# One decoder layer on one core: the first modulation columns, the emptying of banks and the FFN's modulation sums rearranged

## The chip, the core and the metric

The kernel runs on one core of a Trainium2 chip. The metric is the time of the core in microseconds of the device, as the median of several runs; lower is better. One execution is also profiled, and every row below is from that one.

## What is computed

One layer over 512 tokens of width 1024, in float32. A vector c gives six modulation vectors by one product with `w_mod` (1024 x 6144):

```python
mod = silu(c) @ w_mod + b_mod           # sh_m, sc_m, gt_m, sh_f, sc_f, gt_f
h = rms_norm(x, g_mix_norm) * (1 + sc_m) + sh_m
proj = h @ w_in                         # 12 slices: q, k, v of two mixers, an indexer, two gates
o_a = dsa_attention(...)                # each query keeps the 128 keys that the indexer scores highest
o_b = moba_attention(...)               # two blocks of 256 keys
merged = sigmoid(gate_a) * (o_a @ w_br_dsa) + sigmoid(gate_b) * (o_b @ w_br_moba)
x = x + gt_m * (merged @ w_out)
h = rms_norm(x, g_ffn_norm) * (1 + sc_f) + sh_f
x = x + gt_f * ((silu(g) * u) @ w_down) # g, u = halves of h @ w_gate_up; inner width 2816
```

## The kernel before

Every large product is made of three passes on TensorE in a rounded float32 format: high x high, high x low and low x high, where an operand's high part is its rounded copy (made by ScalarE) and its low part the difference (made by VectorE). Weights come from HBM into one of three `st` buffers, always through the queue of SyncE (SP), which takes its transfers in order and waits in order. A weight chunk is 256 rows by 512 columns (24 products of 512 columns, one unit of each half of the chunk); it is cast and split two chunks ahead of its use.

**The opening.** It is written out by hand, in one fixed order for each engine. x comes in four tiles of 128 tokens; each is squared and summed, scaled by its reciprocal root and turned by TensorE (`turn`), one 128-column slice into each of seven banks `xps`. The columns of `w_mod` for the first slice are summed over their 1024 rows: ScalarE takes the first two blocks (`first_products`), VectorE adds further ones (`add_up`), TensorE takes those that `direct` names and then the sum of VectorE (`sum_up`), all into two columns `pc` of one bank, column 1 the scale and column 0 the shift. VectorE makes `acol` (scale) and `mcol` (shift) of them, ScalarE makes the high part of the first slice (`high(0)`), and the products of the first slice begin (`first_group`). From slice 1 on a loop does the same once for each slice k, with the products of slice k-1 ahead of it. `unused_products(n)` issues n products of the identity with itself, of 384 columns, whose result nobody reads; they write columns 128 to 511 of the bank that holds `pc`. `keep` copies a turned slice out of its bank.

**The body.** After the opening a planner in Python (`Clocks`, `step`, `pump`) decides at build time in which order everything else is issued. The products of weight chunks follow a fixed list; each group of four chunks fills four banks, and `fin` (of `v_done`, `raw_done`, `gate_done` and others) empties a bank at the group's last chunk. Side work (rotary tables, indexer, top-k, attention heads, modulation) consists of generators in `tasks`; `step()` runs after every three products (`main3`) and issues each task's next piece if the planner's clocks say that its inputs are ready and that its engines are not more than `slack` ahead of TensorE. `arriving` is the planner's guess of when a transfer lands. `prep` casts and splits a weight chunk.

**The FFN's modulation.** `columns_task` makes four vectors of 512 modulation values as columns (128 partitions x 4 each), with `mod_columns`: `column_sums` accumulates on VectorE into one tile of 128 x 512, `halves` splits it, and TensorE sums over partitions with the tile's 128-column pieces as weights and two columns of ones as the moving operand: eight products of 2 columns. `norm_task` reads the columns first when it prepares the FFN's input.

`out_units` holds the second half of the product with `w_out`; after each tile's last product `residual` empties the bank on VectorE and `norm_task` is spawned.

Of the kernel before, what the change touches and what calls it, by code (L numbers as in the profile page):

```python
# [25 lines left out]
P = 128  # L26
# [87 lines left out]
def layer(ctx, tc, x, vecs, w_mod, w_in, gvecs, w_br_dsa, w_br_moba, w_out, w_gate_up, w_down, cosh, sinh, cosi, sini, out):  # L114
# [6 lines left out]
    wp = ctx.enter_context(tc.tile_pool(name="wp", bufs=3))  # L121
    sm = ctx.enter_context(tc.tile_pool(name="sm", bufs=2))
    pp = ctx.enter_context(tc.tile_pool(name="pp", bufs=1, space=PS))

    NB = {"H": 4, "O": 4, "K": 4, "V": 2, "g": 16, "gu": 2, "s": 3, "pT": 2, "cg": 2}
    uid = [0]
# [161 lines left out]
    with tc.manual_schedule(engines=engines):  # L288
# [13 lines left out]
        junk = t("V", [P, D])  # L302
        xnT = [t("O", [P, 4, S]) for _ in range(2)]
        sums = [None] * NK
        direct = {(0, 1): (6, 7), (0, 0): (4, 5, 6, 7), (1, 1): (6, 7), (1, 0): (6, 7)}

        def blocks(k, m):

# [16 lines left out]
                    ve.scalar_tensor_tensor(dst(j % 2), src(j), cs[:, j:j + 1], dst(j % 2), op0=ALU.mult, op1=ALU.add)  # L325
            ve.tensor_tensor(out=dst(0), in0=dst(0), in1=dst(1), op=ALU.add)

        def sum_up(k, pc, ms=(1, 0)):

            for m in ms:  # L330
                for n, j in enumerate(direct.get((k, m), ())):
                    te.matmul(pc[:, m:m + 1], strips[k][:, m, j, :], cs[:, j:j + 1], start=not n, stop=False)
                te.matmul(pc[:, m:m + 1], sums[k][:, 0, m, :], one, start=(k, m) not in direct, stop=True)

        def high(k, src):
# [40 lines left out]
        def rstd(i, more):  # L376
            ve.tensor_scalar(rs[i], ssx[:, i:i + 1], more, None, op0=ALU.add)
            ge.tensor_tensor(out=rs[i], in0=rs[i], in1=mhalf[:, 0:1], op=ALU.pow)

        for i in range(NT - 1):  # L380
            se.activation(junk, xs[i], AF.Square, scale=D ** -0.5, accum_out=ssx[:, i:i + 1])
            rstd(i, EPS)
            if i < NT - 2:
                scale(i)
                turn(i, range(NK - 1))
                unused_products(3)
        se.activation(junk[:, :512], xs[3][:, :512], AF.Square, scale=D ** -0.5, accum_out=ssx[:, 3:4])
        ve.tensor_tensor_reduce(out=junk[:, 512:], in0=xs[3][:, 512:], in1=xs[3][:, 512:], op0=ALU.mult, op1=ALU.add,
                                scale=1.0 / D, scalar=EPS, accum_out=ssx[:, 4:5])
        rstd(3, ssx[:, 4:5])  # L390
        scale(2)
        scale(3)
        turn(2, range(NK - 1))
        turn(3, (3, 4, 5, 6, 0, 1, 2))
        unused_products(2)
        first_products(0, 1)
        add_up(0, 1)
        sum_up(0, pc, (1,))
        first_products(0, 0)
        add_up(0, 0)  # L400
        sum_up(0, pc, (0,))
        unused_products(6)
        parts = weights_hi(0, (slice(0, 512), slice(512, 512 + N_Q)))
        next(parts)
        keep(3, se.copy)
# [2 lines left out]
        ve.scalar_tensor_tensor(acol[:, 0, 0:1], pc[:, 1:2], gmix[:, 0:1], bmg[:, 0:1], op0=ALU.mult, op1=ALU.add)  # L408
        keep(5, ve.tensor_copy)
        ve.tensor_scalar(mcol[:, 0:1], pc[:, 0:1], bm[:, 0:1], None, op0=ALU.add)  # L410
        high(0, xps[0])
        keep(6, ve.tensor_copy)
        weights_lo(0, slice(0, 512))
# [71 lines left out]
    def spawn(gen, slack=2.0, rank=2, on=busy):  # L485
        tasks.append([gen, (), slack, on, rank])
        tasks.sort(key=lambda task: task[4])

    def step():

        moved = False
        while True:
            hit = False
            for wait in (0.0, 0.15):
                for task in list(tasks):
                    fill = task[4] == 3
                    if wait and (hit or not fill):
                        continue
                    while task in tasks:
                        now = ck.at[PE]  # L500
                        if max(ck.at[e] for e in task[3]) > now + task[2]:
                            break
                        limit = max(now, ck.at[DVE] + 0.12 + wait) if fill else now
                        if not all(w is not None and w <= limit for w in map(when, task[1])):
                            break
                        hit = True
                        try:
                            task[1] = next(task[0]) or ()
                            if not isinstance(task[1], tuple):
                                task[1] = (task[1],)  # L510
                        except StopIteration:
                            tasks.remove(task)
                        if fill:
                            break
            if not hit:
                return moved
            moved = True
# [14 lines left out]
    def need_room(tag):  # L532
        pump(lambda: free[tag])

    def main3(*args):
        mm3(*args)
        step()

    def group(srcs, n, accs_of, mm, order, fin, need=(), change=None):

        accs = {}
        nk = 2 * len(srcs)
        chunks = []
        for c, src in enumerate(srcs):
            def unit(w, ks, js, last, c=c):
                if not accs:
                    accs.update(accs_of())
                for a, b in ([(k, j) for j in js for k in ks] if last else [(k, j) for k in ks for j in js]):
                    mm(accs[b], w[0][:, a], w[1][:, a], 2 * c + a, b, c == 0 and a == 0, 2 * c + a == nk - 1)
                    if last and a == ks[-1]:  # L550
                        fin(b, accs[b])
                        done(accs[b])

            last = c == len(srcs) - 1
            h = (len(order) + 1) // 2
            parts = [((0, 1), order[:h]), ((0, 1), order[h:])] if last else [((0,), order), ((1,), order)]
            units = [lambda w, p=p, unit=unit, last=last: unit(w, p[0], p[1], last) for p in parts]
            chunks.append((lambda src=src, n=n: wload(src, 2, n), units, need, change))
        return chunks

    def drive(chunks, ws, ahead=2):
        sts = {}

        def load(c):
            if c < len(chunks) and chunks[c][0]:
                need_room("st")
                sts[c] = chunks[c][0]()

        def prep(c):
            if c < len(chunks) and chunks[c][0]:  # L570
                st = sts.pop(c)
                if chunks[c][3]:
                    chunks[c][3](st)
                uid[0] += 1
                h, l = [wp.tile(list(st.shape), F32R, name=f"w{q}_{uid[0]}", tag="w" + q) for q in "hl"]
                se.copy(h, st)
                yield h
                ve.tensor_tensor(out=l, in0=st, in1=h.bitcast(F32), op=ALU.subtract)
                done(st)
                ws[c] = h, l  # L580
            load(c + 1)

        load(ahead)
        for c, (load_of, units, need, _) in enumerate(chunks):
            pump(lambda: all(f in ready for f in need) and (not load_of or c in ws))
            for u, unit in enumerate(units):
                unit(ws.get(c))
                if u == 0:
                    spawn(prep(c + ahead), slack=4.0, rank=-1, on=(DVE,))
                    step()  # L590
            ws.pop(c, None)
# [349 lines left out]
    def mod_columns(col0):  # L941

        tile, sums = yield from column_sums(col0, "K")
        parts = yield from halves(sums)
        done(tile)
        yield parts + (room("pstr"),)
        pc = ps("tr", (P, 4, 2))
        for j in range(4):
            for n, part in enumerate(parts):
                te.matmul(pc[:, j, :], part[:, j * P:(j + 1) * P], oner.to_broadcast([P, 2]), start=n == 0, stop=n == 1)  # L950
        j0 = col0 // P
        ve.tensor_tensor(out=mcol[:, j0:j0 + 4], in0=pc[:, :, 0], in1=bm[:, j0:j0 + 4], op=ALU.add)
        done(pc, *parts)

    def mod_rows(acc, col0, tag):

# [14 lines left out]
    def columns_task():  # L971
        yield "idx"
        for part in range(4):
            yield from mod_columns(3 * D + part * 512)
        ve.tensor_scalar(acol[:, 1, :], mcol[:, 32:40], 1.0, None, op0=ALU.add)
        ve.tensor_tensor(out=acol[:, 1, :], in0=acol[:, 1, :], in1=gffn, op=ALU.mult)

# [36 lines left out]
    def br_done(br, half):  # L1014
        def fin(f, acc):
            if not br and not half and not f:
                pump(lambda: len(free["K"]) == 4)
                merged.extend(t("K", [P, 4, S], F32R) for _ in range(4))
            j = 8 * br + 4 * half + f
            pump(lambda: f"gate{j}" in ready)  # L1020
            ve.tensor_tensor(out=gates[j], in0=acc, in1=gates[j], op=ALU.mult)
            if not br:
                spawn(merge(half, f), slack=0.5, rank=0)
            if half and f == 3:
                done(*outs[br])
        return fin
# [131 lines left out]
    def out_units():  # L1158
        units = []
        accs = {}  # L1160
        for i in range(NT):
            for k2 in range(NK // 2):
                def unit(_, i=i, k2=k2):
# [5 lines left out]
                    for k in (2 * k2, 2 * k2 + 1):  # L1169
                        mh, ml = mk(k, i)  # L1170
                        pump(lambda: len(wo) > k)
                        main3(accs[i], mh, ml, wo[k][0][:, 0], wo[k][1][:, 0], k == 0, k == NK - 1)
                    if k2 == NK // 2 - 1:
                        spawn(norm_task(i, residual(accs[i], gtm, i, 1)), slack=4.0, rank=-0.1 * i)
                        done(accs[i])
                        if i == NT - 1:
                            done(*gtm, *(q for hl in wo for q in hl), *merged)
                units.append(unit)
        return units

# [198 lines left out]
```

## Time and profile before

| | |
|---|---|
| median of 3 runs | 797.36 us (797.09 to 797.89) |
| the profiled execution | 797.7 us, of which 795.9 us lie between its first and last instruction |
| mean granted TensorE clock | 0.997 |
| busy share | TensorE 98%, VectorE 60%, ScalarE 46% |
| moved from and to HBM | 100.59 MB, mean 126 GB/s |

The span is what the rows below count in, from the first instruction on. A clock of 1.00 is 2.4 GHz, one of 0.50 is 1.2 GHz. Busy times of TensorE are no measure of its pace, since its products overlap: two products that start 0.23 us apart are each shown as 0.39 us long.

### The profile page before, as it was taken

The numbers are of one execution on the slowest core, as the hardware profiler recorded it, in microseconds if no ns is written. First come the engines' busy times: TensorE is split into PE (matmuls) and PEld (weight loads), VectorE is DVE, ScalarE is ACT, GpSimd is POOL, SyncE is SP. The second block draws the span as 40 slices with busy tenths as digits, with TensorE's granted clock in tenths as the row PEclk, the third lists the DMA queues.
The fourth block names the chain that finished last, engine by engine and source line by source line (L and its number), as shares of the span: only waits on it lengthen the run. The fifth ranks groups of instructions, "written<-read, shape, count | busy, mean of one in ns | idle before, by whom it ended". The sixth has DMA issues, their size and how long they took to land.

```text
span 795.9 us, 10081 instructions
## 1 busy us (share of the span) xinstructions
PE 781.0 (98%) x3743; PEld 648.2 (81%) x3743; DVE 477.4 (60%) x879; ACT 363.5 (46%) x763; POOL 29.1 (4%) x32
## 2 busy tenths in 40 slices
PE   5999999999999999999999999999999999999998
PEld 5887788787888788888888988888888888888886
DVE  4874979998799638638857365233333333644542
ACT  5763579898576777334434323223332322211210
POOL 2000012110020000000000000000000000000000
PEclk9999999999999999999999999999999999999999
DMA  9947343321144444634520176332332332433311
GB/s 323 342 140 225 127 156 83 130 76 58 54 132 142 149 140 158 206 106 141 164 93 20 34 215 207 106 106 90 96 106 86 99 88 71 133 107 109 129 54 53
DMA packets 78036, 100.59 MB, mean 126 GB/s; under 512 B 5980, under 2 KB 46244, under 8 KB 77988
## 3 DMA queue, kind: packets, MB, share of 16 engines
q1 hardware_dynamic: 77988, 99.96, 39.9%
q8 instruction: 29, 0.48, 0.2%
q14 instruction: 19, 0.16, 0.1%
HBM read 97.85 MB, written 2.10 MB: 126 GB/s over the span
## 4 chain that ended last, share of the span: by engine, by line
PE 96%; ACT 2%; DVE 1%; DMA 0%; issue 0%; POOL 0%; SPq 0%; DVEq 0%; ACTq 0%
PE psacc L107 62%; PE pstr L107 16%; PE pspv L107 9%; PE pss L107 9%; DMA O<-in_x_dram 0%; ACT sqj L107 0%; ACT V L107 0%; ACT g L107 0%; ACT H L107 0%; DVE pT L107 0%; DVE score L107 0%; DVE O L107 0%; DVE wl L107 0%; ACT s L107 0%; DVE s L107 0%
## 5 line engine op out<-in xcount | busy, mean ns | idle before, releaser
L107 DVE TENSOR_TENSOR wl<-st,wh 128x1024 fp32r<-128x1024 f32 (+1 forms) x120 | 145.0, 1208 | 123.5 <-ACT wh L107 122.5
L107 ACT CAST wh<-st 128x1024 fp32r<-128x1024 f32 (+1 forms) x120 | 124.4, 1038 | 178.9 <-PE psacc L107 66.7
L107 PE MATMUL psacc<-H,wh 128*128 128x512 f32 x576 | 181.8, 397 | 0.0
L107 PE MATMUL psacc<-wh,H 128*128 128x512 f32 x384 | 130.9, 408 | 3.0 <-ACT H L107 2.1
L107 PEld LDWEIGHTS psacc<-H,wh 128*128 128x128 f32 x576 | 106.8, 188 | 22.9 <-issue 1.4
L107 PE MATMUL psacc<-H,wl 128*128 128x512 f32 x288 | 112.3, 390 | 0.0
L107 PEld LDWEIGHTS psacc<-wh,H 128*128 128x128 f32 x384 | 72.2, 189 | 20.3 <-ACT H L107 2.7
L107 PE MATMUL psacc<-wl,H 128*128 128x512 f32 x192 | 71.9, 395 | 0.0
L107 PEld LDWEIGHTS psacc<-H,wl 128*128 128x128 f32 x288 | 54.1, 188 | 11.6
L107 PE MATMUL pstr<-H,wh 128*128 128x512 f32 (+1 forms) x176 | 54.3, 390 | 0.0
L107 PEld LDWEIGHTS psacc<-wl,H 128*128 128x128 f32 x192 | 36.8, 192 | 7.5 <-issue 1.0
L107 POOL TENSOR_TENSOR m<-m,mhalf 128x4 f32<-128x4 f32 (+1 forms) x24 | 27.3, 1136 | 403.4 <-DVE m L107 355.8
L107 PE MATMUL psacc<-wh,K 128*128 128x512 f32 x128 | 39.8, 389 | 0.0
L107 PE MATMUL psacc<-O,wh 128*128 128x512 f32 x128 | 39.4, 389 | 0.0
L107 PEld LDWEIGHTS pstr<-H,wh 128*128 128x128 f32 (+1 forms) x176 | 32.3, 183 | 7.6
L107 ACT ACTIVATE s<-s,att 128x128 f32<-128x128 f32 (+3 forms) x64 | 34.2, 561 | 2.0 <-DVE att L107 2.0
L107 PE MATMUL pstr<-H,wl 128*128 128x512 f32 (+1 forms) x88 | 34.3, 389 | 0.0
L107 DVE TENSOR_TENSOR s<-psacc,s 128x512 f32<-128x512 f32 x12 | 8.3, 692 | 40.9 <-PE psacc L107 38.7
L107 PEld LDWEIGHTS psacc<-wh,K 128*128 128x128 f32 x128 | 24.0, 188 | 5.1 <-DVE g L107 0.2
L107 PEld LDWEIGHTS psacc<-O,wh 128*128 128x128 f32 x128 | 24.0, 188 | 5.0
L107 DVE TENSOR_TENSOR st<-st,cg 128x1024 f32<-128x1024 f32 x22 | 26.8, 1218 | 0.0
L107 PEld LDWEIGHTS pspv<-pT,V 128*128 128x128 f32 x160 | 21.9, 190 | 6.0 <-DVE O L107 2.5
(236 smaller groups left out, 1342.4 us busy)
## 6 DMA issues: line engine op xcount, KB each, us to landing
st<-in_w_gate_up_dram SPq DMA_DIRECT2D x88, 256.0 KB, 3.2
st<-in_w_in_dram SPq DMA_DIRECT2D x36, 512.0 KB, 3.6
K<-in_w_mod_dram SPq DMA_DIRECT2D x12, 1024.0 KB, 6.5
st<-in_w_down_dram SPq DMA_DIRECT2D x22, 512.0 KB, 3.6
K<-in_w_mod_dram SPq DMA_DIRECT2D x16, 512.0 KB, 6.2
st<-in_w_in_dram SPq DMA_DIRECT2D x16, 256.0 KB, 4.1
st<-in_w_mod_dram SPq DMA_DIRECT2D x8, 512.0 KB, 3.7
O<-in_x_dram SPq DMA_DIRECT2D x4, 512.0 KB, 4.8
```

Source lines behind the costliest of these rows:

```text
L107: inst = f(*args, **kw)
```

## The change

In the opening: fourteen unused products go ahead of x, two instead of three follow each of the first two tiles, the two after the last tile and the six after the sums go, and four stand behind the first shift (`mcol`), ahead of `high(0)`. One more block of the first scale column is summed by TensorE (`direct`), and the direct products of that column are issued ahead of the turning of tiles 2 and 3.

In the body: at a group's last chunk side tasks may run 1 us less far ahead (`held_back`); after a bank's last product `step()` comes behind the bank's emptying, in `group` and in `out_units`; `prep` waits, in the plan, for its weights' landing; `merge` gets a slack of 1.5 in place of 0.5.

In `mod_columns`: the ones are the weights (two columns) and the two halves the moving operand, so two products of 512 columns give the sum as a row; ScalarE copies the row out, one transfer writes it to HBM and another reads it back into the four columns of `mcol`. The bias is added once, after the fourth part, by one instruction that the plan puts at least 8 us behind the landing that it guesses.

```diff
-        direct = {(0, 1): (6, 7), (0, 0): (4, 5, 6, 7), (1, 1): (6, 7), (1, 0): (6, 7)}
+        direct = {(0, 1): (5, 6, 7), (0, 0): (4, 5, 6, 7), (1, 1): (6, 7), (1, 0): (6, 7)}
...
-        def sum_up(k, pc, ms=(1, 0)):
+        def sum_direct(k, pc, m):
+            for n, j in enumerate(direct.get((k, m), ())):
+                te.matmul(pc[:, m:m + 1], strips[k][:, m, j, :], cs[:, j:j + 1], start=not n, stop=False)
+
+        def sum_up(k, pc, ms=(1, 0), begun=False):
...
+        unused_products(14)
         for i in range(NT - 1):
...
-                unused_products(3)
+                unused_products(2)
...
         scale(3)
+        sum_direct(0, pc, 1)
         turn(2, range(NK - 1))
         turn(3, (3, 4, 5, 6, 0, 1, 2))
-        unused_products(2)
         first_products(0, 1)
         add_up(0, 1)
-        sum_up(0, pc, (1,))
+        sum_up(0, pc, (1,), begun=True)
         first_products(0, 0)
         add_up(0, 0)
         sum_up(0, pc, (0,))
-        unused_products(6)
...
         ve.tensor_scalar(mcol[:, 0:1], pc[:, 0:1], bm[:, 0:1], None, op0=ALU.add)
+        unused_products(4)
         high(0, xps[0])
...
+    held_back = [0.0]
...
-                        if max(ck.at[e] for e in task[3]) > now + task[2]:
+                        if max(ck.at[e] for e in task[3]) > now + task[2] - held_back[0]:
...
     def main3(*args):
         mm3(*args)
-        step()
+        if not emptied_next[0]:
+            step()
...
+                held_back[0] = 1.0 if last else 0.0
                 for a, b in ([(k, j) for j in js for k in ks] if last else [(k, j) for k in ks for j in js]):
+                    emptied_next[0] = last and a == ks[-1]
                     mm(accs[b], w[0][:, a], w[1][:, a], 2 * c + a, b, c == 0 and a == 0, 2 * c + a == nk - 1)
-                    if last and a == ks[-1]:
+                    if emptied_next[0]:
+                        emptied_next[0] = False
                         fin(b, accs[b])
                         done(accs[b])
+                        step()
...
+                yield st
                 uid[0] += 1
...
-        parts = yield from halves(sums)
+        hi, lo = yield from halves(sums)
+        yield hi, lo, room("pstr")
+        pc = ps("tr", (2, 512))
+        te.matmul(pc, oner.to_broadcast([P, 2]), hi, start=True, stop=False)
+        te.matmul(pc, oner.to_broadcast([P, 2]), lo, start=False, stop=True)
+        done(hi, lo)
+        yield pc
+        row = sums[0:1, :]
+        se.copy(row, pc[0:1, :])
+        done(pc)
+        yield sums
+        j0 = col0 // P
+        turned = dp.tile([1, 512], F32, name=f"turned{j0}")
+        nc.sync.dma_start(turned, row)
+        nc.sync.dma_start(mcol[:, j0:j0 + 4], turned.rearrange("o (a p) -> p (o a)", p=P), allow_slow_non_contiguous=True)
+        arriving(mcol, 512)
         done(tile)
-        yield parts + (room("pstr"),)
-        pc = ps("tr", (P, 4, 2))
-        for j in range(4):
-            for n, part in enumerate(parts):
-                te.matmul(pc[:, j, :], part[:, j * P:(j + 1) * P], oner.to_broadcast([P, 2]), start=n == 0, stop=n == 1)
-        j0 = col0 // P
-        ve.tensor_tensor(out=mcol[:, j0:j0 + 4], in0=pc[:, :, 0], in1=bm[:, j0:j0 + 4], op=ALU.add)
-        done(pc, *parts)
...
+        landed = ck.ready[mcol.tensor.name][0] + 8.0
+        yield lambda: landed
+        ve.tensor_tensor(out=mcol[:, 24:40], in0=mcol[:, 24:40], in1=bm[:, 24:40], op=ALU.add)
...
-                spawn(merge(half, f), slack=0.5, rank=0)
+                spawn(merge(half, f), slack=1.5, rank=0)
...
-                        main3(accs[i], mh, ml, wo[k][0][:, 0], wo[k][1][:, 0], k == 0, k == NK - 1)
+                        (mm3 if k == NK - 1 else main3)(accs[i], mh, ml, wo[k][0][:, 0], wo[k][1][:, 0], k == 0, k == NK - 1)
...
                             done(*gtm, *(q for hl in wo for q in hl), *merged)
+                        step()
```

## Rows read from the trace of the kernel before

**Rows 1.** The page: busy time by engine, and the chain that ended last.

```profile
PE 781.0 (98%) x3743; PEld 648.2 (81%) x3743; DVE 477.4 (60%) x879; ACT 363.5 (46%) x763; POOL 29.1 (4%) x32
...
PE 96%; ACT 2%; DVE 1%; DMA 0%; issue 0%; POOL 0%; SPq 0%; DVEq 0%; ACTq 0%
```

**Rows 2.** Busy time by stretch: engines in order, then clock, DMA share, GB/s.

```profile
19.40:22.80 3.40, 3.36 (x8) 2.61 (x9) 3.37 (x7) 3.40 (x7) 0.00 (x0) 0.54 1.11 369
...
100.00:200.00 100.00, 99.24 (x515) 81.83 (x514) 89.58 (x233) 84.93 (x254) 15.49 (x11) 1.00 0.31 98
```

**Rows 3.** Waits of TensorE over the span: total us, times, longest.

```profile
PE pstr L107 <- DVE m L107: 4.5, 1, 4.5
...
PE psacc L107 <- ACT H L107: 2.1, 2, 1.9
PE psacc L107 <- DVE s L107: 1.0, 1, 1.0
PE psacc L107 <- ACT g L107: 0.8, 1, 0.8
```

**Rows 4.** Timeline of TensorE in the opening: start, us, what, idle before.

```profile
10.60 1.06 PE L107 MATMUL psacc<-identr,O 128*128 128x128 f32 x4
...
12.97 1.04 PE L107 MATMUL psacc<-identr,O 128*128 128x128 f32 x8
...
16.00 0.36 PE L107 MATMUL pstr<-one,gu 128*128 128x1 f32 x2
16.23 1.31 PE L107 MATMUL pstr<-identr 128*128 128x384 f32 x6
...
19.44 1.87 PE L107 MATMUL psacc<-wh,H 128*128 128x512 f32 x4 [1.91 <-ACT H L107]
...
23.66 1.08 PE L107 MATMUL psacc<-wh,H 128*128 128x512 f32 x4
24.58 0.40 PE L107 MATMUL pspv<-wl,H 128*128 128x512 f32 x1
...
28.11 1.19 PE L107 MATMUL psacc<-wh,H 128*128 128x512 f32 x4 [0.19 <-ACT H L107]
```

**Rows 5.** Timeline of VectorE in the opening, and one row of ScalarE.

```profile
11.47 1.14 DVE L107 SCALAR_TENSOR_TENSOR gu<-K,cs,gu 128x128 f32<-128x128 f32 x4
...
13.49 0.29 DVE L107 TENSOR_TENSOR gu<-gu 128x128 f32<-128x128 f32 x1
17.58 0.22 DVE L107 SCALAR_TENSOR_TENSOR acol<-pstr,cols,bmg 128x1 f32<-128x1 f32 x1 [3.79 <-PE pstr L107]
...
18.31 0.21 DVE L107 TENSOR_SCALAR mcol<-pstr,cols 128x1 f32<-128x1 f32 x1
...
23.38 0.43 DVE L107 TENSOR_TENSOR gu<-gu 128x256 f32<-128x256 f32 x1
...
18.61 0.78 ACT L107 ACTIVATE H<-pstr,mcol,acol 128x512 fp32r<-128x512 f32 x1 [3.31 <-DVE mcol L107]
```

**Rows 6.** Timeline of TensorE where one part's columns are summed.

```profile
158.92 1.03 PE L107 MATMUL pstr<-oner,gu 128*128 128x2 f32 x8
159.81 0.48 PE L107 MATMUL psacc<-wh,H 128*128 128x512 f32 x1
```

**Rows 7.** Timelines of ScalarE and VectorE around two waits of TensorE.

```profile
151.72 1.30 ACT L107 ACTIVATE g<-g,m 128x128 f32<-128x128 f32 x4
...
153.42 1.09 ACT L107 COPY g<-psacc 128x512 f32<-128x512 f32 x2
...
428.83 1.37 DVE L107 TENSOR_SCALAR pT<-pstr,acol,mcol 128x128 f32<-128x128 f32 x4 [1.35 <-PE pstr L107]
430.12 0.68 DVE L107 TENSOR_TENSOR s<-psacc,cg 128x512 f32<-128x512 f32 x1
```

**Rows 8.** Transfers by tile: count, KB each, median us from issue to landing.

```profile
K<-in_w_mod_dram SPq DMA_DIRECT2D x16, 512.0 KB, 6.2
...
out_dram<-V SPq DMA_DIRECT2D x7, 256.0 KB, 2.0
```

More of the change, by code (lines that the diff above doesn't have):

```diff
@@ L123, in layer @@
     pp = ctx.enter_context(tc.tile_pool(name="pp", bufs=1, space=PS))
+    dp = ctx.enter_context(tc.tile_pool(name="dp", bufs=1, space=bass.MemoryType.DRAM))
     NB = {"H": 4, "O": 4, "K": 4, "V": 2, "g": 16, "gu": 2, "s": 3, "pT": 2, "cg": 2}
@@ L326, in add_up @@
             ve.tensor_tensor(out=dst(0), in0=dst(0), in1=dst(1), op=ALU.add)
-        def sum_up(k, pc, ms=(1, 0)):
+        def sum_direct(k, pc, m):
+            for n, j in enumerate(direct.get((k, m), ())):
+                te.matmul(pc[:, m:m + 1], strips[k][:, m, j, :], cs[:, j:j + 1], start=not n, stop=False)
+        def sum_up(k, pc, ms=(1, 0), begun=False):
             for m in ms:
-                for n, j in enumerate(direct.get((k, m), ())):
-                    te.matmul(pc[:, m:m + 1], strips[k][:, m, j, :], cs[:, j:j + 1], start=not n, stop=False)
+                if not begun:
+                    sum_direct(k, pc, m)
                 te.matmul(pc[:, m:m + 1], sums[k][:, 0, m, :], one, start=(k, m) not in direct, stop=True)
@@ L533, in need_room @@
         pump(lambda: free[tag])
+    emptied_next = [False]
     def main3(*args):
         mm3(*args)
-        step()
+        if not emptied_next[0]:
+            step()
     def group(srcs, n, accs_of, mm, order, fin, need=(), change=None):
```

## The prediction, made before the changed kernel was run

> **What bounds the kernel now.** I read the page first: TensorE is busy for 781.0 of 795.9 us, and the chain that ended last runs through it for 96% of the span [rows 1]. A change can then win time in two ways only: by taking products off TensorE, or by closing the few stretches in which it stands still or runs slowly. So the next view is the waits of TensorE, which are few enough to name all that matter [rows 3]: 4.5 us until x is there, 2.1 us (1.9 us of it in one piece) for the high part of the first slices, 1.0 us for VectorE and 0.8 us for ScalarE to empty a bank. The view by stretch adds what a wait list can't show: in the 3.4 us behind the longest of these waits but the first, the granted clock is 0.54, half speed for nearly all of it, while eight products run [rows 2]. The timelines then say who holds whom at each of these places [rows 4, 5, 7].
>
> **The opening.** The chain there is: sums of VectorE, last sum on TensorE, `acol`, a copy, `mcol`, `high(0)`, first product. VectorE has its last sum ready at 13.49 + 0.29 = 13.78 us [rows 5]. TensorE makes the last of the sums only at 16.00, because it turned x at half speed: four pieces took 1.06 us at 10.60, eight took 1.04 us at 12.97 [rows 4]. And `acol` starts not at 16.36, when the sums are done, but at 17.58, with the end of the six unused products (16.23 + 1.31 = 17.54), which write the same bank [rows 4, 5]. From `acol` to the first product the way is fixed: 17.58 to 19.44, 1.86 us.
>
> What the change does to it. At full speed an unused product takes at most 1.31 / 6 = 0.22 us [rows 4], at half speed 0.44, so fourteen need 3.1 to 6.1 us; they lie in the 4.5 us of idle ahead of x [rows 3], and turning starts at most 1.6 us late. Nothing hangs on that: VectorE is still scaling tiles 2 and 3 until 11.47 us, when it goes over to the sums [rows 5]. TensorE has then been busy from about 3 us on in place of 7.4. Before, its clock rose between 10.60 and 12.97; four us sooner it is up well ahead of tile 2. Turning then ends at 12.4 to 13.2 us. VectorE adds three blocks in place of four, 1.14 / 4 = 0.29 us less, so its last sum is ready at 13.5. TensorE's own part of the shift column is eight passes, 0.9 us by the eight of two columns at 158.92 [rows 6], and the two last sums take 0.36 us each [rows 4]: the bank is done at 14.3 to 14.9 us. With no unused products in between, `acol` starts there, 2.7 to 3.3 us before 17.58; I take 3.1. ScalarE doesn't hold `high(0)`: it had waited 3.31 us for `mcol` at 18.61, so it was free at 15.3 already [rows 5], and now it is sooner. The first product comes at 16.3 us in place of 19.44.
>
> The four unused products behind `mcol` must wait for it, because they write the bank that it reads. They take 4 x 0.22 = 0.9 us at most and lie beside `high(0)`, 0.78 us: at full speed they cost 0.1 us or nothing, at half speed 0.4 to 1 us. TensorE's longest stop is then 1.0 us, from 14.5 to 15.4, where it was 1.9.
>
> If the clock stays up, the eight slow products win too: four took 1.87 us at 19.44 and 1.08 us at 23.66, so 1.6 us for eight [rows 2, 4]. Not all of it counts, because the first slice's products end in the modulation sums of slice 1, for which VectorE is late next. Its sum was ready at 23.38 + 0.43 = 23.81, 5.3 us after `mcol` (18.31 + 0.21) [rows 5]; TensorE came to it three products after 24.58, at 25.3, and began slice 1 at 28.11, 2.8 us later [rows 4]. Now `mcol` ends at 15.4 and the sum is there at 20.7 to 21.1; TensorE has done its 18 products, at 0.23 us, by 16.3 + 4.1 = 20.4 and its direct passes at 20.9. It waits 0.3 us or less and begins slice 1 at 23.2 to 23.7. **Term 1: 4.4 us**, between 2.7 (3.1 less 0.4 for slow unused products, all else as before) and 4.8.
>
> **Loads.** Moving 4.4 us forward asks the same of the transfers. One slice needs 1.5 MB (1 MB of `w_mod`, 0.5 MB of `w_in`), and TensorE spends 21 x 0.23 us and four passes on it, 5.3 us: 285 GB/s. The queue brings 369 GB/s here [rows 2], so it gains on TensorE with each slice. I price this at nothing; if loads were the bound, all of term 1 but 1 us could go.
>
> **The modulation as rows.** Eight products of 2 columns hold TensorE from 158.92 to 159.81, 0.89 us [rows 6]. Two of 512 columns at 0.23 us apart (0.92 us for four, 23.66 to 24.58) take 0.46 us [rows 4]; weights of two columns instead of 128 can make that only less. **Term 2: 4 x 0.43 = 1.7 us.** ScalarE gets a copy of one row per part, 0.55 us at most by its copies of a whole bank (1.09 for two [rows 7]), VectorE loses a small addition; neither sets the end [rows 1].
>
> The turn over HBM has no row like it. The first transfer writes 2 KB, the second fetches 512 values of 4 bytes. Below, a landing takes 2.0 us, as the output's 256 KB do; above, 6.2 us as the loads of `w_mod` do behind one another [rows 8], or 13 us if all 512 pieces went through one engine: 512 KB of `w_mod` are 1024 pieces of 512 bytes and pass in 1.4 us at 369 GB/s, 64 pieces for each of 16 engines, 0.022 us a piece, 11 us for 512, and 2.0 for the landing. I take 2 to 3 us, since neither moves more than 2 KB. SP holds its queue for the first of the two: for ScalarE's copy, then for the landing, because the second reads what the first wrote. Behind it stand weight loads, some 3 to 6 us late. They are cast two chunks ahead of use, and a chunk is 24 products, 5.5 us, and longer with side work; so TensorE doesn't see it, though ScalarE's cast may. The last part's landing holds one addition on VectorE, which the plan puts 10.7 us or more behind the issue (0.7 + 2.0 guessed, 8 added). At 13 us VectorE would stop for 2 us, still within a chunk.
>
> The Trainium skill, in "DMA: Bandwidth & Descriptors", section "Rules for kernel authors", speaks against this turn: it wants the hardware's transpose and not a plain transfer with rearranged access, and gives 19 times as the difference. By that, as an estimate, 2.0 us become 38 us. No row of this trace has pieces of 4 bytes, so none confirms or excludes it.
>
> **Banks emptied first.** At 152.9 us ScalarE scales four heads (151.72, 1.30 us) and makes a cast before it copies the bank out (153.42); TensorE waits 0.8 us. At 429.6 VectorE makes four pieces of `pT` (428.83, 1.37 us) before `residual` takes the bank (430.12): 1.0 us [rows 3, 7]. Both are the order that `emptied_next` and the moved `step()` turn round, 1.8 us to win. What is late next is the side work that is put back; its engines are 85 to 90% busy between 100 and 200 us [rows 2], so holding it back by 1 us at each group's end bunches it, and the plan of the whole body is drawn anew. My bound for new waits is 0 to 1.8 us, the size of what now exists; I take half. `prep`'s wait and `merge`'s slack change the plan only, and are priced with it. **Term 3: 1.0 us**, between 0 and 1.8.
>
> **Sum.** 4.4 + 1.7 + 1.0 = 7.1 us off the profiled execution's 797.7 us (1.8 of them around the span) is 790.6; the median of the runs lies 0.3 lower than the profiled one: 790.3 us.
>
> **Rivals.**
> *The clock falls in spite of the unused products.* TensorE stops for 1.0 us at about 14.5; before, the clock fell after 1.9 us of nothing. For: the sums around the stop are products of one column. Against: such sums stood directly ahead of 16.23 before, and six unused products then ran at full speed [rows 4]. Some 1.3 us of term 1 go: 791.6 us.
> *The gain of the opening is given back*, to late loads or to new waits for banks in the redrawn plan. For: a DMA share of 1.11, engines 85 to 90% busy [rows 2]. Against: the rates above, and that only two such waits are worth naming now. It leaves 3 to 4 us: 794 us.
> *The turn over HBM lands late.* The bias addition on VectorE waits for it, and behind it stand the low parts of the weights and much of the emptying of banks. Each us over 10.7 stops VectorE; after 5.5 us more, TensorE. It decides at 10.7 + 5.5 + 7.1 = 23 us: with a longer landing the kernel is slower than before, at 30 us with 790.3 + 30 - 16.2 = 804 us. Against: the worst order that rows allow is 13 us. The estimate of 38 us from the Trainium skill's "DMA: Bandwidth & Descriptors" would give 812 us.
> *The change doesn't do what it says*: `acol` waits for something else than the unused products. Nothing speaks for it but that the wait is named "PE" only. Then terms 2 and 3 remain and 1.5 us of clock: 793.5 us.
>
> **Chances.** Forecast 0.58, falling clock 0.20, given back 0.12, no earlier `acol` 0.06, late landing 0.04 (half of it over the point where it decides). The range reaches from all terms at their best, 4.8 + 1.7 + 1.8 = 8.3 us off (789.1, and 0.4 for the spread of the runs), to the gain given back: 788.7 to 794.0. A measurement here tells 0.2%, 1.6 us, from no change, so faster means under 795.8: 0.95; same 0.03; slower 0.02.
>
> **What would show it.** `acol` at 14.3 to 14.9 us, directly behind the last sum; first product at 16.3; a clock of 1.00 from there on; slice 1's products at about 23.7; four pairs of 512-column products on two columns of ones; no wait of TensorE of 0.7 us or more behind 30 us. I am wrong if the first product comes after 17.5, if its four take 1.8 us, if VectorE stands still ahead of the bias addition, or if new waits for banks add up to over 2 us.

## The result, and the profile after

The changed kernel needs 791.64 us (median of six runs, 789.93 to 793.03), the kernel before 797.23 us on the same chip (796.47 to 797.89): a ratio of 0.9929, with an interval of 0.9917 to 0.9942. That is 1.3 us above the forecast, and faster by 0.7%. The profiled execution is the quickest of the six: 789.93 us, 787.9 us of it between its first and last instruction, mean clock 0.999. The other five had mean clocks of 0.996 to 0.998.

The page's busy times and chain [rows 1], and then the waits of TensorE (total us, times, longest) [rows 3], now read:

```profile
PE 777.4 (99%) x3729; PEld 646.0 (82%) x3729; DVE 477.3 (61%) x875; ACT 363.9 (46%) x767; POOL 30.4 (4%) x32
...
PE 97%; DMA 1%; ACT 0%; DVE 0%; SPq 0%; issue 0%; DVEq 0%
```

```profile
PE pstr L107 <- DMA pT<-in_vecs_dram: 2.6, 1, 2.6
PE pspv L107 <- DVE O L107: 2.3, 1, 2.3
PE pstr L107 <- DVE mcol L107: 1.0, 1, 1.0
PE pstr L107 <- DMA K<-in_w_mod_dram: 0.6, 1, 0.6
PE psacc L107 <- ACT H L107: 0.2, 1, 0.2
PE pstr L107 <- DVE O L107: 0.2, 1, 0.2
```

The two waits for a bank are gone, and so is the 1.9 us for `high(0)`. A line has come that was not there: 2.3 us in one piece, for an attention head's output `O` from VectorE.

The opening, TensorE [rows 4], VectorE [rows 5] and the stretch behind the first product [rows 2]:

```profile
6.99 0.52 PE L107 MATMUL pstr<-identr 128*128 128x384 f32 x1
7.31 0.44 PE L107 MATMUL pstr<-identr,O 128*128 128x128 f32 x1
...
9.57 0.60 PE L107 MATMUL psacc<-identr,O 128*128 128x128 f32 x4
...
14.55 0.36 PE L107 MATMUL pstr<-one,gu 128*128 128x1 f32 x2
15.95 0.96 PE L107 MATMUL pstr<-identr 128*128 128x384 f32 x4 [1.04 <-DVE mcol L107]
16.83 1.20 PE L107 MATMUL psacc<-wh,H 128*128 128x512 f32 x4
...
23.89 1.19 PE L107 MATMUL psacc<-wh,H 128*128 128x512 f32 x4 [0.19 <-ACT H L107]
```

```profile
14.96 0.22 DVE L107 SCALAR_TENSOR_TENSOR acol<-pstr,cols,bmg 128x1 f32<-128x1 f32 x1 [0.74 <-PE pstr L107]
...
15.69 0.21 DVE L107 TENSOR_SCALAR mcol<-pstr,cols 128x1 f32<-128x1 f32 x1
...
20.77 0.42 DVE L107 TENSOR_TENSOR gu<-gu 128x256 f32<-128x256 f32 x1
```

```profile
16.00:20.00 4.00, 4.00 (x18) 3.21 (x19) 3.97 (x8) 3.48 (x6) 0.00 (x0) 1.00 1.12 360
```

`acol` stands directly behind the last sum, the clock is 1.00, the first product comes at 16.83 us and slice 1 begins at 23.89 us, 4.22 us sooner than before. Counting the products with weights (`wh` or `wl`) in both traces, the changed kernel is 4.20 us ahead at the 60th and still at the 240th, 6.71 us ahead once attention is over (the 1080th, 344 us before), and 7.99 us from the 1500th to the end.

One pair of the new products, with its neighbours [rows 6], and the two transfers of the turn [rows 8]:

```profile
218.06 0.62 PE L107 MATMUL pstr<-gu,oner 128*2 128x512 f32 x2
218.52 0.61 PE L107 MATMUL psacc<-H,wh 128*128 128x512 f32 x2
```

```profile
turned<-K SPq DMA_DIRECT2D x4, 2.0 KB
mcol<-turned SPq DMA_DIRECT2D x4, 2.0 KB, 2.2
```

This pair holds TensorE for 0.46 us, where eight small products held it 0.89. All four pairs together, from the start of each to the next product, take 2.2 us, and the 32 small products before took 3.8. The turn lands in 2.2 us (median; 2.1 to 3.0).

And the new wait, in the order of time, all engines (SPq is SP's queue):

```profile
270.67 0.56 ACT L107 COPY K<-pstr 1x512 f32<-1x512 f32 x1
...
271.25 0.24 SPq L975 DMA_DIRECT2D turned<-K  x1
...
272.40 0.37 SPq L976 DMA_DIRECT2D mcol<-turned  x1
...
274.57 0.17 DVE L107 TENSOR_TENSOR mcol<-mcol,cols 128x16 f32<-128x16 f32 x1 [2.90 <-DMA mcol<-turned]
...
275.74 0.27 DVE L107 TENSOR_TENSOR O<-pspv,O 128x128 fp32r<-128x128 f32 x1
...
276.07 0.71 PE L107 MATMUL pspv<-pT,V 128*128 128x128 f32 x4 [2.27 <-DVE O L107]
```

The bias addition is already at the head of VectorE's queue when the last row has just been copied out. It stands there for 2.90 us, from 271.67 us on; two small instructions on `acol`, a reciprocal, a search for maxima and `O` of a head wait behind it, and TensorE for `O`.

### The profile page after: what moved, and what is told of

Read it like the earlier page. It is cut to its first block, busy times and chain, and to the rows that moved or that the text cites. A ratio compares the mean times of both kernels' runs of the same rounds, so it can differ in the third digit from the quotient of the medians.

```text
span 787.9 us, 10050 instructions
## 1 busy us (share of the span) xinstructions
PE 777.4 (99%) x3729; PEld 646.0 (82%) x3729; DVE 477.3 (61%) x875; ACT 363.9 (46%) x767; POOL 30.4 (4%) x32
## 4 chain that ended last, share of the span: by engine, by line
PE 97%; DMA 1%; ACT 0%; DVE 0%; SPq 0%; issue 0%; DVEq 0%
PE psacc L107 63%; PE pstr L107 16%; PE pspv L107 9%; PE pss L107 9%; DMA K<-in_w_mod_dram 1%; DMA mcol<-turned 0%; SPq L218 0%; DMA turned<-K 0%; DVE O L107 0%; ACT H L107 0%; ACT s L107 0%; DVE m L107 0%; ACT K L107 0%; SPq L202 0%; DVE V L107 0%
## 5 line engine op out<-in xcount | busy, mean ns | idle before, releaser
L107 PE MATMUL psacc<-wh,H 128*128 128x512 f32 x384 | 126.3, 400 | 0.2 <-ACT H L107 0.2
L107 ACT ACTIVATE s<-s,att 128x256 f32<-128x256 f32 (+3 forms) x64 | 34.0, 563 | 5.4 <-DVE att L107 5.1
L107 ACT ACTIVATE s<-psacc 128x512 f32<-128x512 f32 x12 | 7.2, 598 | 48.0 <-PE psacc L107 48.0
```

Source lines behind the costliest of these rows:

```text
L107: inst = f(*args, **kw)
```

## The experiments

Every kernel is compared with the kernel before on the same chip, where that one had a median of 797.71 us (e1 to e4), 797.69 us (e5 to e8) and 797.38 us (e9 to e11). "Opening", "rows" and "plan" are the three parts of the diff above.

**e1: the opening's edits alone** (down to `unused_products(4)` in the diff; everything below as before).

> The kernel before with the edits of the opening alone. Theory (the terms add up; the opening's 4.2 us are kept to the end): slice 1 begins at 23.9 us in place of 28.1, nothing of it is lost behind, 4.2 us less than before where the clock holds and some 2.7 us where it falls in the opening; median 793.0 to 794.5. Rival (the 4.2 us are given back later, because side work and loads in the body are as late as before): 795 or more, with slice 1 at 23.9 all the same.

Measured: 794.72 us, ratio 0.9968 (0.9958 to 0.9977), 3.0 us gained: between the two expectations, 0.2 us above the first one's range. In the profiled execution the first product comes at 16.43 us, but at half speed (timeline, then the stretch):

```profile
15.51 1.12 PE L107 MATMUL pstr<-identr 128*128 128x384 f32 x4 [1.03 <-DVE mcol L107]
16.43 2.03 PE L107 MATMUL psacc<-wh,H 128*128 128x512 f32 x4
```

```profile
16.20:19.60 3.40, 3.40 (x10) 2.54 (x9) 3.37 (x7) 2.83 (x6) 0.00 (x0) 0.50 1.12 353
```

The same 1.0 us stop stands ahead of it as in the changed kernel's profile, where the clock held. So the first rival (the clock falls in spite of the unused products) does happen, and costs 1.0 us: the lead is 3.2 us at the 60th product in place of 4.2. It is 3.1 us at the end, so the opening's gain isn't given back. Two of the twelve executions had a mean clock of 1.000; they took 793.20 and 793.66 us.

**e2: the rows alone** (the `mod_columns` and bias hunks).

> The kernel before with the modulation as rows alone. Theory (the sums on TensorE take 1.5 us less, and the bias addition stops VectorE, and TensorE behind it, for 2.3 us, because its place in the plan doesn't follow the transfer): a wait of TensorE of about 2 us behind a wait of VectorE for the transfer into mcol; 0.8 us slower than before to 0.5 faster, 796.7 to 798. Rival (the stop at 273 us is an accident of the whole change's plan): no such wait, 1.5 us faster, 795.7.

Measured: 805.57 us, ratio 1.0100 (1.0087 to 1.0113): 7.9 us slower, and both expectations failed: the stop is there, but it is not all. Waits of TensorE, then the stretch behind the stop:

```profile
PE pspv L107 <- DVE O L107: 3.4, 3, 3.0
PE psacc L107 <- ACT g L107: 3.3, 4, 1.3
...
PE pstr L107 <- DVE gu L107: 1.1, 2, 0.6
PE psacc L107 <- DVE s L107: 1.0, 1, 1.0
```

```profile
317.20:320.60 3.40, 3.40 (x12) 2.90 (x12) 1.88 (x4) 1.23 (x3) 0.00 (x0) 0.50 0.00 0
```

VectorE waits 3.28 us for `mcol<-turned` at 313.09 us, TensorE 3.0 us for the head behind it; then TensorE runs at half speed for 3.4 us, which loses another 1.7. Waits for ScalarE to empty a bank (`ACT g`) grow from 0.8 to 3.3 us, and 1.1 us for the halves are new. Together 3.4 + 1.7 + 2.5 + 1.1 less the 1.6 that the products save: 7.1 of the 7.9 us.

**e3: the plan's edits alone** (`held_back`, `emptied_next`, `prep`, `merge`, `out_units`).

> The kernel before with the plan's edits alone (banks emptied first, side work held back, the waits of prep and the slack of merge). Theory: the two waits for banks of 0.8 and 1.0 us go, with some small costs between side products: 1.8 to 2.8 us less, 794.4 to 795.4. Rival (held-back work bunches): new waits of TensorE of over 0.5 us, 796.5 or more.

Measured: 794.81 us, ratio 0.9968 (0.9956 to 0.9980), 2.9 us gained, as expected. No wait for a bank is left; behind the opening only two short ones for `gu`, 0.6 us together.

The three parts alone give -3.0, +7.9 and -2.9 us, which add up to +2.0; together they give -5.6. What the rows do to the plan depends on the plan's edits, so their price alone isn't their price in the change.

**e4: the changed kernel with the bias added later.** The 8 us are counted from the furthest of the plan's engines, not only from its guess of the landing.

```diff
-        landed = ck.ready[mcol.tensor.name][0] + 8.0
+        landed = max(ck.ready[mcol.tensor.name][0], *ck.at.values()) + 8.0
```

> The changed kernel with the bias addition planned 8 us behind the plan's own present, not behind its guess for the transfer alone. Theory (the wait of 2.3 us at 273 us hangs on that guess): the wait is gone, 2.3 us less than the changed kernel, span 785.6 where the clock holds, median 789.4; the runs still differ by 2 us or more, since the clock is what spreads them, with the lower mean clock in the longer runs. Rival (the spread of the changed kernel's runs is that wait's, as the transfer's landing varies): the runs lie within 1 us.

Measured: 787.62 us (786.63 to 788.49), ratio 0.9877 (0.9864 to 0.9889), 4.0 us less than the change. In the profile (waits of TensorE, all of 0.2 us or more; then VectorE) no wait behind the opening is left, and the addition, now at 280.49 us, waits for nothing:

```profile
PE pstr L107 <- DMA pT<-in_vecs_dram: 2.5, 1, 2.5
PE pstr L107 <- DMA K<-in_w_mod_dram: 1.5, 1, 1.5
PE pstr L107 <- DVE mcol L107: 1.0, 1, 1.0
PE psacc L107 <- ACT H L107: 0.2, 1, 0.2
```

```profile
280.49 0.17 DVE L107 TENSOR_TENSOR mcol<-mcol,cols 128x16 f32<-128x16 f32 x1
```

The stop had cost 2.3 us in the profiled execution, and the median foretold from that was 789.4. That 4.0 go with it left two theories for the rest: the clock falls behind that stop in most executions, or what spreads the runs is the clock in the opening. e5 and e6 tell them apart.

**e5 and e6: six more unused products in another bank**, between the last sum and `mcol`, so that TensorE doesn't stop there; e5 with the late bias, e6 with the bias where the change has it.

```diff
         keep(3, se.copy)
+        spare = xps[3].rearrange("p (a d) -> p a d", a=4)
+        for _ in range(6):
+            te.matmul(spare[:, 1:], identr, identr.unsqueeze(1).to_broadcast([P, 3, P]), start=True, stop=True)
         keep(4, se.copy)
```

> The kernel with the late bias, and six unused products more in the opening, in a bank that is free by then, so that TensorE doesn't stop while `acol` and `mcol` are made. Theory 1 (in most runs the clock falls in the opening, as the profile of the opening alone shows at 16.2 us, and this is what spreads the runs): it holds now in every run; the runs lie within 1 us and the median 1 us below the one with the late bias alone, 786.6. Theory 2 (the clock falls at the stop at 273 us instead, which the late bias has taken away): nothing changes, 787.6, spread 1.9 us.

> The changed kernel with the six unused products more, its bias addition where it was. Theory 1 (the clock falls in the opening): the median comes down to the profiled run of the changed kernel, 789.9. Theory 2 (the stop at 273 us makes it fall): the median stays at 791.6 and a profile of an execution as slow as that shows the half-speed stretch behind the stop.

Measured: e5 787.30 us (786.76 to 790.40; 0.9879, 0.9862 to 0.9895), not to be told from e4; e6 791.77 us (0.9926, 0.9914 to 0.9939), not to be told from the change. In e6's profile the clock is up throughout the opening, and TensorE stops at 273.8 us for 2.8 us as it does in the change. The stretches of the stop, behind it, and behind that:

```profile
273.80:277.30 3.50, 0.71 (x5) 0.41 (x4) 1.83 (x10) 1.21 (x2) 0.00 (x0) 0.99 0.60 128
277.30:280.70 3.40, 3.40 (x11) 2.60 (x10) 1.57 (x7) 2.42 (x7) 0.00 (x0) 0.50 0.46 177
280.70:284.00 3.30, 3.30 (x19) 2.84 (x19) 3.30 (x9) 0.97 (x4) 0.00 (x0) 1.00 0.22 36
```

Half speed for 3.4 us loses 1.7: with the stop's 2.3 to 2.8 these are the 4 us. So the stop at 273 us, and the clock that falls behind it, set the changed kernel's median. Its own profiled execution kept full speed there, and by the mean clocks it is the only one of six, which is why its profile alone doesn't show this. No slow execution of the changed kernel itself was profiled; that it is like e6's is argued from the medians and the mean clocks.

Two things stay open. One of e5's four executions took 790.40 us at a mean clock of 0.996, though e5 has neither the stop at 273 us nor the one in the opening. And e1 and e4 have the same opening, but the mean clock was below 1.000 in ten of e1's twelve executions and in one of e4's four.

**e7: the rows alone, with the late bias** (e2 and e4's line).

> The kernel before with the modulation as rows alone, and the bias addition planned late. Theory (of the 8 us that the rows alone lost, the stop for the transfer, 3.0 us, and the half speed behind it, 1.7 us, hang on the addition's place): 4.7 us less than the rows alone, 801, with four waits of 0.3 to 1.3 us for banks and the split left. Rival (the whole loss hangs on that one place): 796.2, 1.5 us faster than before.

Measured: 800.62 us, ratio 1.0037 (1.0024 to 1.0051): 5.0 us less than e2, as the theory said. The addition waits for nothing (319.81 us). What keeps this kernel slower than before is the other part, the waits for `ACT g`, 3.3 us still, and 1.2 us for `gu`.

**e8: the late bias, and six unused products back ahead of `acol`, in the bank of the sums.**

```diff
         sum_up(0, pc, (0,))
+        unused_products(6)
```

> The kernel with the late bias, and the six unused products put back between the modulation sums and `acol`, in the bank that holds the sums. Theory (`acol` starts with the end of whatever TensorE writes in that bank): `acol` 1.0 us later (6 x 0.16) behind the last sum, and the first product too; 1 us slower, or less where the clock, which holds in more runs now, gives some of it back: 787.6 to 788.6. Rival (`acol` follows the sums alone): `acol` within 0.1 us of the last sum's end.

Measured: 789.06 us, ratio 0.9891 (0.9878 to 0.9905), 1.4 us more than e4, with intervals that overlap, and 0.5 us above the theory's range. TensorE and VectorE in its profile:

```profile
14.09 0.36 PE L107 MATMUL pstr<-one,gu 128*128 128x1 f32 x2
14.32 1.29 PE L107 MATMUL pstr<-identr 128*128 128x384 f32 x6
16.65 1.65 PE L107 MATMUL pstr<-identr 128*128 128x384 f32 x4 [1.04 <-DVE mcol L107]
```

```profile
15.65 0.22 DVE L107 SCALAR_TENSOR_TENSOR acol<-pstr,cols,bmg 128x1 f32<-128x1 f32 x1 [1.89 <-PE pstr L107]
```

`acol` starts with the end of the unused products, 1.2 us behind the sums: it waits for whoever writes its bank last, though they write other columns. In e5 six such products stand behind the same sums (14.14 + 0.36 = 14.50 us) in another bank, and `acol` doesn't wait for them:

```profile
14.36 1.29 PE L107 MATMUL psacc<-identr 128*128 128x384 f32 x6
14.54 0.22 DVE L107 SCALAR_TENSOR_TENSOR acol<-pstr,cols,bmg 128x1 f32<-128x1 f32 x1 [0.74 <-PE pstr L107]
```

So the fourth rival (it waits for something else) falls. Whether the chip asks for that wait, or only the order that the program gives, the runs don't show.

**e9: the late bias, without the fourteen unused products ahead of x.**

> The changed kernel with the late bias, without the fourteen unused products ahead of x. Theory (they bring the rise of the clock forward, and turning at half speed is all that they spare): tiles 0 and 1 are turned at half speed again and the clock rises between 10 and 12.5 us; the turning ends some 0.3 to 0.6 us later, acol comes at 14.9 to 15.5 us, and the kernel needs 788.0 to 788.8 us, 0.4 to 1.2 more than with them. Rival one (they carry the opening): acol at 16 us or later, 789.5 us or more. Rival two (the sums of VectorE set the opening anyway): acol at 14.5 as before, 787.4 to 787.8 us.

Measured: 788.85 us (787.63 to 791.89), ratio 0.9899 (0.9882 to 0.9915), 1.2 us more than e4, with intervals that overlap. In its profile `acol` comes at 15.58 us, and tiles 0 and 1 are turned at half the pace again (four pieces in 1.06 us, where the change took 0.60):

```profile
10.27 1.06 PE L107 MATMUL psacc<-identr,O 128*128 128x128 f32 x4
...
15.18 0.36 PE L107 MATMUL pstr<-one,gu 128*128 128x1 f32 x2
16.58 0.97 PE L107 MATMUL pstr<-identr 128*128 128x384 f32 x4 [1.04 <-DVE mcol L107]
```

The last sum is 0.6 us later than in the change (15.18 to 14.55), and the lead at the 60th product 3.6 us to its 4.2. So the work ahead of x brings 0.6 of the 4.2 us where the clock holds. The rest, read from the traces of before and after: the sums end 1.45 us sooner (14.91 for 16.36; these 0.6 are part of it), `acol` follows them at once in place of 1.2 us later (e8), and the first slice's products at full speed take 1.6 us less. Three of e9's six executions have a mean clock of 1.000 (787.63 to 788.07 us), the other three 0.997 to 0.998 (789.62 to 791.89), for which nothing was profiled.

**e10 and e11: the rows with the late bias, and half of the plan's edits each**: e10 with the order at a bank's end (`emptied_next`, `step()` behind the emptying, `out_units`) and the wait in `prep`, e11 with `held_back` and `merge`'s slack.

> The kernel before with the sums as rows and the late bias, and of the plan's edits the order at a bank's end (emptying ahead of step, in group and in out_units) and the wait in prep for the weights' landing; no holding back by 1 us, merge with its old slack. Theory (the 3.3 us of waits for ScalarE to empty a bank, which the rows brought into the plan of before, are the same thing as the three bank waits of before, and the order at the bank's end takes both away): TensorE waits for ACT g at most 0.5 us, 796 to 797 us, against 800.6 without these edits. Rival (holding back side work by 1 us is what takes them away): waits for ACT g of 2 us or more stay, 799 us or more.

> The kernel before with the sums as rows and the late bias, and of the plan's edits only the holding back of side work by 1 us at a group's last chunk and merge's slack of 1.5. Theory (order at the bank's end decides): waits for ACT g of 2 us or more stay, 799 to 801 us. Rival (holding back decides): ACT g under 0.8 us, 797 to 798 us.

Measured: e10 795.18 us (0.9970, 0.9959 to 0.9981), e11 792.91 us (0.9943, 0.9930 to 0.9956), against 800.62 for e7: both less than either expectation had. Waits of TensorE behind the opening, e10 and then e11:

```profile
PE psacc L107 <- DVE K L107: 0.8, 1, 0.8
PE psacc L107 <- ACT V L107: 0.2, 1, 0.2
```

```profile
PE psacc L107 <- DVE s L107: 1.0, 1, 1.0
```

Neither has a wait for `ACT g`. The theory that the order at the bank's end decides fell with e11: holding back 1 us of side work (with `merge`'s slack) removes the same waits, without touching that order, and gains more. Each half is enough for these; the old 1.0 us for `s` needs the order, which e11 lacks. Why e11 is 2.3 us better than e10 is in part open: in the profiled executions (794.06 and 791.98 us) e11 is 0.8 us ahead at the 60th product already, though the two openings are the same, and 0.8 us is e10's wait for `K`.

## Why the prediction was right, and where it was wrong

**The account.** The profiled execution is 7.8 us quicker (797.7 to 789.93), where the sum said 7.1. But the median lies 1.7 us above this execution, where I took it 0.3 below, as before. The mean clock was 0.999 in the one and 0.996 to 0.998 in the others. That the median still lies within 1.3 us of the forecast is in part luck: the stop at 273 us and the half speed behind it, 4.0 us with e4 as the measure, stood in no term, and 0.8 us of bank waits and some 2.4 us from the redrawn plan made up for most of it.

**Term 1** (4.4 us): 4.2, kept to the end. `acol` came at 14.96 us, just past the 14.3 to 14.9 foretold, the first product at 16.83 for 16.3, the stop ahead of it was the 1.0 us foretold, and slice 1 began at 23.89 for 23.2 to 23.7. TensorE waited 0.6 us for a block of `K`, which it hadn't before; in e4 it is 1.5 us, and the lead at the 60th product 3.7. VectorE's sum for slice 1 was ready at 21.19 us (20.77 + 0.42), TensorE came to the passes ahead of it at 21.06: nothing waited, as said. Behind the opening loads took nothing back (e1's lead is constant). The rival of the falling clock was real in e1 and e8, but in the changed kernel it isn't what moves the median (e6). One reading of the prediction goes further than its rows: that the clock rose between 10.60 and 12.97 us is read from the pace of the turned pieces. The profile's column of the granted clock is 1.00 there in the kernel before, with the slow pieces in it (stretch as in [rows 2]), and 1.00 in e9 too:

```profile
7.00:13.00 6.00, 5.55 (x24) 5.37 (x25) 5.00 (x15) 4.01 (x11) 2.31 (x3) 1.00 1.08 362
```

The halved pace, and that it ends sooner with the fourteen products, is measured; that it is the granted clock isn't shown.

**Term 2** (1.7 us): 1.6. In the body, 32 products of two columns took 3.8 us; the eight that replace them took 2.2. SP stood in four pieces ahead of the transfer that writes the row, 24.1 us together and 8.6 at the longest, until ScalarE had made the copy; I had taken 3 to 6 us. TensorE got no wait for weights from it, as said.

**Term 3** (1.0 us, between 0 and 1.8): both bank waits went and no new one came, 1.8 us. I had taken half, against a redrawn plan. The redrawn plan gave more instead: of the 2.5 us by which the lead grows between the 240th and the 1080th product, 1.6 are term 2's and 0.8 a bank wait, and the new stop took 2.3, so 2.4 us more come from products that follow each other more closely amid the side work. e3 shows part of it without the rows: from the 60th to the 1500th product it gains 2.8 us, where the two bank waits are 1.8 and its new waits for `gu` take 0.6 back, so 1.6 us are of this kind. What the rows add to it no run isolated.

**The step that failed** is "the plan puts 10.7 us or more behind the issue". VectorE stood still ahead of the bias addition, which I had named as a sign of being wrong, and TensorE waited for over 0.7 us behind 30 us, where I had foretold no such wait. The plan did hold the addition 8 us, but behind its own guess, and that guess counts from the plan's last transfer and the last use of `mcol`. It knows nothing of ScalarE's copy of the row, nor of SP's queue, which waits for the copy and then for the first transfer. In the run the guess lay so early that the addition was at the head of VectorE's queue at 271.67 us, 0.7 us before the transfer into `mcol` was issued (272.40). "After 5.5 us more, TensorE" fell with it: I had put weights and banks behind VectorE there, but a head's `O` stood behind the addition too, with TensorE's next product waiting for it, so that 2.90 us of VectorE became 2.27 us of TensorE at once.

**The third rival** had the place right and the condition wrong. I let a landing of 23 us decide; landings were 2.2 us in the change and 2.2 to 3.5 over all ten kernels that have the rows (medians; 5.0 the longest single one, in e2 and e7), and what decided was when the addition was issued. At the worst place tried (e2) the same landing belongs to a kernel 7.9 us slower, 5.0 of it by the place alone (e7). My 2 to 3 us for the landing was right for the change. The Trainium skill's rule in "DMA: Bandwidth & Descriptors", "Rules for kernel authors" (19 times for a rearranged transfer, 38 us as an estimate here) isn't borne out as that estimate for 512 values: the ten profiles have medians of 2.2 to 3.5 us. The factor itself stands against the hardware's transpose, which no run here uses.

**Better than both.** The change with e4's one line takes 787.62 us, 4.0 us less than the change and 10.1 less than before; with e5's products too, 787.30.

## What to carry to other kernels

When a queue that runs in order gets an instruction that waits for a transfer, the time of the transfer is the smaller question: ask from what event its place is counted, and whether that event is known to whoever plans the order. Look then at what stands behind it, for one stop of TensorE costs itself and the slow stretch that can follow. And when several edits redraw one plan, their times alone don't add: rows alone cost 7.9 us, yet are part of the best version.

## What the runs showed that I had not expected

- A stop of TensorE of 1.0 us (between `mcol`'s sums and the first products) was followed by half speed in the profiled executions of e1 and e8, and not in those of the change, e4 and e9; a stop of 2.3 us in the middle of full work was survived in the profiled run of the change, 2.8 us (e6) and 3.0 us (e2) were not. The half-speed stretch was 3.4 us long in e1, e2, e6 and e8, and 6.8 us in e3's opening.
- 512 values of 4 bytes each, turned over HBM, land in 2.2 us (median of the change), little more than the 2.0 us of 256 KB of output [rows 8]; in e2 and e7 one landing took 5.0.
